# The second part of a quarter of the FFN's gate and up weights: an accumulating DMA from SBUF to SBUF in place of a DVE subtract

## The chip, the cores and the metric

The program runs on one core of a Trainium2 chip. The metric is device time in microseconds of one execution. A core has TensorE (PE in the profile; its weight loads are listed as PEld), VectorE (DVE), ScalarE (ACT), GpSimd (POOL) and SyncE (SP). SP and POOL issue DMAs, all of which run on the core's 16 DMA engines.

## The reference

One decoder layer on 256 tokens of 2048 features in float32. Cut to its flow:

```python
proj = rms_norm(x, norm1_w) @ w_in                 # q, k, v, xr, yr, g_att, g_lru
att = attention(q, k, v)                           # 16 heads of 128, one block of 256 keys, causal
lru = rglru_branch(xr, yr, ...)                    # conv, gates, a scan over tokens
merged = sigmoid(g_att) * (att @ w_proj_attn) + sigmoid(g_lru) * (lru @ w_proj_lru)
x = x + merged @ w_out
h2 = rms_norm(x, norm2_w)
x = x + (silu(h2 @ w_ffn_gate) * (h2 @ w_ffn_up)) @ w_ffn_down     # 2048 -> 5632 -> 2048
```

## The kernel before

Every projection is computed from two parts of each operand: a first part rounded to the type `float32r`, and a second part that holds what the rounding left. Three of the four products of parts are formed (first by first, first by second, second by first) and added in PSUM.

The weights stream from HBM in pieces of 512 rows by 512 columns (1 MB), in the order of their use: 292 pieces, numbered from 0. SP loads a piece into one of four buffers `w_raw` (line 101). Pieces 160 to 247 are the FFN's gate and up weights, 22 blocks of 512 columns with four pieces each, gate and up blocks in turn; pieces 248 to 291 are the down weights.

Each piece is split in two halves (`s` = 0 and 1: its first and last 256 rows) by `split`. For a half, ACT writes the first part to `w_hi` (line 107), and DVE subtracts it from the raw weights to give the second part `w_lo` (line 108). `w_hi` and `w_lo` have four buffers each, given out in turn, two to a piece. So a piece takes the buffers of the piece two before it, and each becomes free when TensorE has used it for the last time.

From piece 48 on, the products are formed with the weight's parts stationary (`features_first`, lines 661 and 662). One piece is sixteen pairs of matmuls: the first part of the weight against both parts of the activations (512 columns), then its second part against their first part (256 columns):

```python
for g in range(2):
    mine = [(k, f) for k in range(KT) for f in fs if f // 2 == g]
    for k, f in mine:
        hi, lo = (p[:, k % 2, f * P:(f + 1) * P] for p in parts[n][k // 2])
        ...
        pe.matmul(o, hi, a[:, :, k, :], ...)
        pe.matmul(o[:, 0, :], lo, a[:, 0, k, :], ...)
```

With four row chunks k and four column groups f, two of them for each g, pairs 1 to 4 use half 0, pairs 5 to 8 half 1, pairs 9 to 12 half 0 and pairs 13 to 16 half 1.

The order on each engine is the order in which this code is written. The loop over pieces writes, for piece n: SP's load of piece n + 3, the split of piece n + 1, the matmuls of piece n, and then work that is due beside the projections (a list of tasks with due times in pieces): evacuating PSUM (lines 304 and 305), the SiLU and its product (lines 602 to 616), the parts of the result `mid` (lines 297 and 298), and norms. A load waits until the raw buffer's last reader is done. GpSimd has next to no work in the FFN: four stores of the first residual sum to HBM (`x1d`, line 584) just before and at the beginning, and two small operations of the second norm (lines 192 and 193).

Of the kernel before, what the change touches and what calls it, by code (L numbers as in the profile page):

```python
# [10 lines left out]
F32 = mybir.dt.float32  # L11
F32R = mybir.dt.float32r
AF = mybir.ActivationFunctionType
OP = mybir.AluOpType
# [8 lines left out]
EPS = 1e-6  # L23
CB = 512          # columns of one block of a projection
KT = 4            # chunks of 128 rows in one loaded piece of a weight
NB = D // CB
NF = DFF // CB
SCALE = HD ** -0.5
MASKED = 1e30

# columns of `vecs`, 16 each (feature = column * 128 + partition)
V_N1, V_N2, V_CW, V_CB, V_BA, V_BX, V_LAM = 0, 16, 32, 96, 112, 128, 144
V_QN, V_KN = 160, 161
NV = 162


@with_exitstack
def layer(ctx: ExitStack, tc: tile.TileContext, x, xT, vecs, w_in, w_rg_a, w_rg_x,
# [16 lines left out]

# [1 line left out]
    pieces = []     # (source, first row chunk, first column)  # L57

# [3 lines left out]

    plan = []       # (kind, index, source of the left operand)

# [25 lines left out]
    raw, parts = {}, {}  # L90
# [19 lines left out]
    def split(n, step=2):  # L110
        if n >= len(pieces):
            return
        parts[n] = []
        for s in range(2):
            r = raw[n][:, 2 * s:2 * s + 2, :]
            hi = wp.tile([P, 2, CB], F32R, name="w_hi", bufs=4)
            lo = wp.tile([P, 2, CB], F32R, name="w_lo", bufs=4)
            parts[n].append((hi, lo))
            if step == 2:
                halves_of(r, hi, lo)  # L120
        if step == 2:
            del raw[n]

# [1 line left out]
    first = const.tile([P, 1], F32, name="first")  # L125
# [10 lines left out]

# [1 line left out]
    hT = [act_block(f"h{c}", "hT") for c in range(NB)]  # L138
# [14 lines left out]

    # the first pieces come chunk by chunk, so that TensorE starts early
    src0 = load(0)
# [14 lines left out]

    # identity, distances
    ones = const.tile([P, P], F32, name="ones")
# [16 lines left out]
    def rsqrt_mean(name, ss, n, width, where=small):  # L189
        """(ss / n + EPS) ** -0.5"""  # L190
        r = where.tile([P, width], F32, name=name)
        pool.tensor_scalar(r, ss, 1.0 / n, EPS, op0=OP.mult, op1=OP.add)
        pool.tensor_tensor(r, r, mhalf[:, :width], op=OP.pow)
        return r
# [3 lines left out]
    def rows_of(r):  # L198
        """[token, half] -> [128 times the same, token]: a task for TensorE, then a copy"""
        box = const.tile([P, T], F32, name="rb")  # L200

        def on_pe():
            t = aux()
            for h in range(2):
                pe.transpose(t[:, h * P:(h + 1) * P], r[:, h:h + 1].to_broadcast([P, P]), ident)
            later(1, lambda: act.activation(box, t[:, :T], AF.Copy))
        later(1, on_pe, True)
        return box

    def square(c, src, tags, name):  # L210
        """adds the squares of a block to those of the blocks before; the last leads to the norm"""
        if c == 0:
            st["sq"] = feat_tile(tags[0], "sq", tags[2])
            act.activation(st["sq"], src, AF.Square)
        else:
            q = feat_tile(tags[1], "sqj", tags[2])
            act.activation(q, src, AF.Square)
            dve.tensor_tensor(st["sq"], st["sq"], q, op=OP.add)
        if c == NB - 1:
            norm(name)  # L220
# [19 lines left out]

    # softplus(-lambda) = max(-lambda, 0) + 2 atanh(e / (2 + e)), e = exp(-|lambda|)
    cpos = const.tile([P, 16], F32, name="cpos")
# [20 lines left out]

# [1 line left out]
    tasks = []      # [slot, order, on TensorE, function]  # L265
    now = [0]
    order = [0]
# [18 lines left out]
    def transposed(src):  # L286
        """[token, half, 512 features] -> PSUM [feature, 4, token]"""
        t = aux()
        tv = t.rearrange("p (k h t) -> p k h t", k=KT, h=2)
        for k in range(KT):  # L290
            for h in range(2):
                pe.transpose(tv[:, k, h, :], src[:, h, k * P:(k + 1) * P], ident)  # L292
        return t

    def parts_of(dst, src):
        """dst [128, 2, 4, 256] from src [128, 4, 256]"""
        act.activation(dst[:, 0], src, AF.Copy)
        later(1, lambda: dve.tensor_tensor(dst[:, 1], src, dst[:, 0].bitcast(F32), op=OP.subtract))

    def gather(acc, dst, then):  # L300
        """dst [128, 4, 256] from the two sums of each feature"""
        def half(g):
            d = dst[:, 2 * g:2 * g + 2]
            act.activation(d, acc[g][:, :, 1, :], AF.Copy)
            dve.tensor_tensor(d, acc[g][:, :, 0, :], d, op=OP.add)
        later(0, lambda: half(0))
        later(1, lambda: (half(1), then()))
# [15 lines left out]

# [1 line left out]
    def qk_done(kind, b, acc):  # L325
# [37 lines left out]
    def scores(b):  # L363
# [44 lines left out]
        def turn(z, pair):  # L408
            t = aux().rearrange("p (a n) -> p a n", a=2)
            for a in range(2):  # L410
                hd = 2 * pair + a
                # keys of the first half: queries of both halves; keys of the second: queries of it
                pe.transpose(t[:, a, :P], z[:, hd, :P], ident)  # L413
                pe.transpose(t[:, a, P:2 * P], z[:, hd, P:2 * P], ident)  # L414
                pe.transpose(t[:, a, 2 * P:3 * P], z[:, hd, 2 * P:], ident)  # L415
# [28 lines left out]

# [1 line left out]
    sg = {}  # L446
# [32 lines left out]

# [1 line left out]
    lru = {}  # L481

    def xr_done(b, acc):
# [53 lines left out]
        def factor(g, at):  # L537
            # 1 - a^2 = tanh(-log a) (1 + a^2)
            dve.tensor_tensor(g[:, 0], at[:, 0], at[:, 0], op=OP.mult)
            dve.scalar_tensor_tensor(at[:, 1], g[:, 0], 1.0, at[:, 1], op0=OP.add, op1=OP.mult)  # L540
            dve.tensor_tensor(u, u, g[:, 1], op=OP.mult)
            later(1, lambda: act.activation(at[:, 1], at[:, 1], AF.Sqrt))
            later(2, lambda: scan(at))
# [20 lines left out]

# [1 line left out]
    x1d = dram.tile([P, NB, KT, T], F32, name="x1d")  # L566
# [26 lines left out]

# [1 line left out]
    ff = {}  # L595
# [43 lines left out]

# [1 line left out]
    def tokens_first(acc, a, n, first, last):  # L641
        """acc [token, half, column]: the left operand's parts are stationary"""
        for k in range(KT):
# [8 lines left out]
    def features_first(acc, a, n, first, last, fs=range(KT)):  # L652
        """acc[g] [column, 2, 2, token]: the weight's parts are stationary; its first part meets both parts
        of the activations in one product, and the two sums are added in the end"""
        for g in range(2):
# [84 lines left out]
```

## Time and profile before

| | |
|---|---|
| time of three runs | median 1689.32 us (1688.47 to 1690.04) |
| the profiled execution: its span, first to last instruction (the page gives no other time of it) | 1686.6 us |
| PE busy, instructions | 1676.7 us (99%), 9276 |
| PEld busy | 1455.4 us (86%) |
| DVE busy | 1040.0 us (62%) |
| ACT busy | 827.9 us (49%) |
| POOL busy | 27.7 us (2%) |
| moved by DMA | 320.30 MB, mean 190 GB/s |

Busy time says how long an engine had an instruction running. A busy engine is not by that the bound: the chain that ended last and the idle time before each group of instructions say who waits for whom. A DMA's time from issue to landing is listed for each issuing line. The DMA share is the mean busy share of the 16 engines.

### The profile page before, as it was taken

How to read it: one execution, taken by the hardware profiler on the slowest of the kernel's cores; microseconds unless marked ns; L12 is line 12 of the kernel's file. 1: busy time of each engine (PE TensorE's matmuls, PEld its weight loads, DVE VectorE, ACT ScalarE, POOL GpSimd, SP SyncE). 2: the span in 40 equal slices, each digit the busy share in tenths (PEclk: the TensorE clock that was granted, in tenths of full speed). 3: DMA queues.
4: the chain of work that ended last, by engine and by line, in shares of the span. 5: the costliest groups of instructions: out<-in, count | busy, mean ns of one | idle time of the engine just before them, and what ended most of it. 6: DMA issues, size and time to landing. Idle time of an engine off the chain costs nothing.

```text
span 1686.6 us, 22468 instructions
## 1 busy us (share of the span) xinstructions
PE 1676.7 (99%) x9276; PEld 1455.4 (86%) x9276; DVE 1040.0 (62%) x1064; ACT 827.9 (49%) x960; POOL 27.7 (2%) x35
## 2 busy tenths in 40 slices
PE   8999999999999999999999999999999999999999
PEld 6888888888888888888888888888888888888887
DVE  6565656655556867768666656666666666554444
ACT  6544554544445665756445444444444444443332
POOL 0100101000000000000000000000000000000000
PEclk9999999999999999999999999999999999999999
DMA  8554545555555555555557655555556555565662
GB/s 306 190 179 155 177 169 174 170 173 182 190 198 175 187 184 203 187 175 177 198 188 245 216 189 186 200 180 194 192 184 199 181 193 192 184 223 188 213 218 82
DMA packets 166294, 320.30 MB, mean 190 GB/s; under 512 B 5296, under 2 KB 15664, under 8 KB 166192
## 3 DMA queue, kind: packets, MB, share of 16 engines
q1 hardware_dynamic: 165328, 316.51, 55.6%
q0 software_dynamic: 576, 2.10, 0.3%
q8 instruction: 72, 1.18, 0.3%
q10 hardware_dynamic: 288, 0.26, 0.0%
q14 instruction: 30, 0.25, 0.0%
HBM read 314.66 MB, written 4.19 MB: 189 GB/s over the span
## 4 chain that ended last, share of the span: by engine, by line
PE 99%; DMA 0%; ACT 0%; SPq 0%; DVE 0%; issue 0%
PE acc L661 53%; PE acc L662 27%; PE acc L649 5%; PE acc L650 5%; PE acc L648 5%; PE aux L515 1%; PE aux L292 0%; PE aux L372 0%; PE aux L431 0%; DMA xc<-in_xT 0%; PE aux L433 0%; PE aux L371 0%; PE aux L415 0%; PE aux L413 0%; PE aux L414 0%; SPq L158 0%
## 5 line engine op out<-in xcount | busy, mean ns | idle before, releaser
L108 DVE TENSOR_TENSOR w_lo<-w_raw,w_hi 128x1024 fp32r<-128x1024 f32 (+1 forms) x586 | 711.9, 1221 | 575.8 <-ACT w_hi L107 575.7
L107 ACT ACTIVATE w_hi<-w_raw 128x1024 fp32r<-128x1024 f32 (+1 forms) x586 | 619.0, 1058 | 757.0 <-PE acc L661 548.5
L661 PE MATMUL acc<-h2T,w_hi 128*128 128x512 f32 x1408 | 488.9, 392 | 0.0
L662 PE MATMUL acc<-h2T,w_lo 128*128 128x256 f32 x1408 | 394.3, 280 | 0.0
L661 PE MATMUL acc<-hT,w_hi 128*128 128x512 f32 x1024 | 360.9, 397 | 0.0
L661 PEld LDWEIGHTS acc<-h2T,w_hi 128*128 128x128 f32 x1408 | 263.4, 187 | 58.1
L662 PE MATMUL acc<-hT,w_lo 128*128 128x256 f32 x1024 | 286.3, 280 | 0.0
L662 PEld LDWEIGHTS acc<-h2T,w_lo 128*128 128x128 f32 x1408 | 266.1, 189 | 0.0
L661 PE MATMUL acc<-mid,w_hi 128*128 128x512 f32 x704 | 244.1, 391 | 0.0
L661 PEld LDWEIGHTS acc<-hT,w_hi 128*128 128x128 f32 x1024 | 192.1, 188 | 45.2
L662 PE MATMUL acc<-mid,w_lo 128*128 128x256 f32 x704 | 197.1, 280 | 0.0
L662 PEld LDWEIGHTS acc<-hT,w_lo 128*128 128x128 f32 x1024 | 193.2, 189 | 0.3
L648 PE MATMUL acc<-w_hi,hT 128*128 128x512 f32 x384 | 153.9, 401 | 5.5 <-ACT w_hi L107 5.4
L661 PEld LDWEIGHTS acc<-mid,w_hi 128*128 128x128 f32 x704 | 131.6, 187 | 28.9
L649 PE MATMUL acc<-w_lo,hT 128*128 128x512 f32 x384 | 151.0, 393 | 0.8 <-DVE w_lo L108 0.8
L650 PE MATMUL acc<-w_hi,hT 128*128 128x512 f32 x384 | 150.7, 392 | 0.0
L662 PEld LDWEIGHTS acc<-mid,w_lo 128*128 128x128 f32 x704 | 133.1, 189 | 0.0
L648 PEld LDWEIGHTS acc<-w_hi,hT 128*128 128x128 f32 x384 | 72.8, 190 | 20.9 <-ACT w_hi L107 6.5
L661 PE MATMUL acc<-attT,w_hi 128*128 128x512 f32 x256 | 90.5, 399 | 0.0
L661 PE MATMUL acc<-merged,w_hi 128*128 128x512 f32 x256 | 90.5, 399 | 0.0
L661 PE MATMUL acc<-lruT,w_hi 128*128 128x512 f32 x256 | 90.3, 398 | 0.1
L649 PEld LDWEIGHTS acc<-w_lo,hT 128*128 128x128 f32 x384 | 72.7, 189 | 16.5 <-DVE w_lo L108 2.0
(166 smaller groups left out, 1303.8 us busy)
## 6 DMA issues: line engine op xcount, KB each, us to landing
w_raw<-in_w_in SPq DMA_DIRECT2D x110, 1024.0 KB, 5.0
w_raw<-in_w_ffn_gate SPq DMA_DIRECT2D x44, 1024.0 KB, 5.0
w_raw<-in_w_ffn_up SPq DMA_DIRECT2D x44, 1024.0 KB, 5.0
w_raw<-in_w_ffn_down SPq DMA_DIRECT2D x44, 1024.0 KB, 5.0
w_raw<-in_w_proj_attn SPq DMA_DIRECT2D x16, 1024.0 KB, 5.0
w_raw<-in_w_proj_lru SPq DMA_DIRECT2D x16, 1024.0 KB, 4.9
w_raw<-in_w_out SPq DMA_DIRECT2D x16, 1024.0 KB, 5.1
xb<-in_xT SPq DMA_DIRECT2D x4, 512.0 KB, 7.9
```

Of the source, the lines that this page charges most:

```text
L107: act.activation(hi, r, AF.Copy)
L108: dve.tensor_tensor(lo, r, hi.bitcast(F32), op=OP.subtract)
L515: pe.matmul(t[:, n * T:(n + 1) * T], wg[:, i, n, :], u[:, n, :], start=True, stop=True, skip_group_check=True)
L648: pe.matmul(o, ah, hi, start=(first and k == 0), stop=False)
L649: pe.matmul(o, ah, lo, start=False, stop=False)
L650: pe.matmul(o, al, hi, start=False, stop=(last and k == KT - 1))
L661: pe.matmul(o, hi, a[:, :, k, :], start=start, stop=False, skip_group_check=True)
L662: pe.matmul(o[:, 0, :], lo, a[:, 0, k, :], start=False, stop=stop, skip_group_check=True)
```

## The change

In `split`, the odd-numbered pieces of the gate and up weights (44 of 88) are handled differently. Their half 1 comes first, before half 0, also in the order in which buffers are given out. For half 1, ACT writes the rounded weights with the sign reversed into `w_lo`, then the rounded weights into `w_hi`; then GpSimd issues a DMA that adds the raw weights to `w_lo` (source and destination both in SBUF, 128 partitions of 4 KB). The result is raw minus rounded, as before. Half 0 of these pieces and all other pieces are handled as before. Comments were taken out of the file, and some lines have other numbers: ACT's copy and DVE's subtract are now lines 108 and 109, the two new copies lines 123 and 124, the new DMA line 125.

```diff
+FIRST_FFN = (7 * NB + 3 * NB) * 4
...
     def split(n, step=2):
         if n >= len(pieces):
             return
-        parts[n] = []
-        for s in range(2):
+        parts[n] = [None, None]
+        beside = FIRST_FFN <= n < FIRST_FFN + 2 * NF * KT and n % 2 == 1
+        for s in (1, 0) if beside else (0, 1):
             r = raw[n][:, 2 * s:2 * s + 2, :]
             hi = wp.tile([P, 2, CB], F32R, name="w_hi", bufs=4)
             lo = wp.tile([P, 2, CB], F32R, name="w_lo", bufs=4)
-            parts[n].append((hi, lo))
-            if step == 2:
+            parts[n][s] = (hi, lo)
+            if beside and s == 1:
+
+                act.activation(lo, r, AF.Copy, scale=-1.0)
+                act.activation(hi, r, AF.Copy)
+                pool.dma_start(lo.bitcast(F32), r, accum_op=OP.add)
+            elif step == 2:
                 halves_of(r, hi, lo)
```

On ACT, this is the stretch around the first up block in the kernel before. `fu` and `fg` are copies out of PSUM, `fs` is the sigmoid, `mid` the first part of a result:

```order
L304 ACTIVATE fu<-acc 128x512
L107 ACTIVATE w_hi<-w_raw 128x1024 x2
L304 ACTIVATE fu<-acc 128x512
L603 ACTIVATE fs<-fg 128x1024
L107 ACTIVATE w_hi<-w_raw 128x1024 x6
L297 ACTIVATE mid<-fu 128x1024
L304 ACTIVATE fg<-acc 128x512
```

The same stretch of ACT with the change:

```order
L311 ACTIVATE fu<-acc 128x512
L123 ACTIVATE w_lo<-w_raw 128x1024
L124 ACTIVATE w_hi<-w_raw 128x1024
L108 ACTIVATE w_hi<-w_raw 128x1024
L311 ACTIVATE fu<-acc 128x512
L610 ACTIVATE fs<-fg 128x1024
L108 ACTIVATE w_hi<-w_raw 128x1024 x2
L123 ACTIVATE w_lo<-w_raw 128x1024
L124 ACTIVATE w_hi<-w_raw 128x1024
L108 ACTIVATE w_hi<-w_raw 128x1024 x3
L304 ACTIVATE mid<-fu 128x1024
L311 ACTIVATE fg<-acc 128x512
```

An odd piece now has three copies on ACT in place of two, and the first of them (line 123) is the one that the new DMA waits for.

On POOL, the end of the program in the kernel before has the last operations of the query and key norms (`rq`), the four stores and the second norm (`rstd`):

```order
L192 TENSOR_SCALAR rq<-ss 128x8
L193 TENSOR_TENSOR rq<-rq,mhalf 128x8
L584 DMA x1d<-xb 128x1024 x4
L192 TENSOR_SCALAR rstd_7744<-ss_7742 128x2
L193 TENSOR_TENSOR rstd_7744<-rstd_7744,mhalf 128x2
```

The same stretch of POOL with the change:

```order
L591 DMA x1d<-xb 128x1024 x3
L125 DMA w_lo<-w_raw 128x1024
L591 DMA x1d<-xb 128x1024
L125 DMA w_lo<-w_raw 128x1024
L199 TENSOR_SCALAR rstd_7746<-ss_7744 128x2
L200 TENSOR_TENSOR rstd_7746<-rstd_7746,mhalf 128x2
L125 DMA w_lo<-w_raw 128x1024 x42
```

Two of the 44 new DMAs stand ahead of the second norm's operations, the first of them ahead of the last store.

## Rows read from the trace of the kernel before

**Rows 1.** The page: busy time of the engines, and for 40 equal slices of the span the granted clock of TensorE and the DMA engines' busy share, in tenths.

```profile
PE 1676.7 (99%) x9276; PEld 1455.4 (86%) x9276; DVE 1040.0 (62%) x1064; ACT 827.9 (49%) x960; POOL 27.7 (2%) x35
...
PEclk9999999999999999999999999999999999999999
DMA  8554545555555555555557655555556555565662
```

**Rows 2.** The page: shares of the chain that ended last, by engine and by line.

```profile
PE 99%; DMA 0%; ACT 0%; SPq 0%; DVE 0%; issue 0%
PE acc L661 53%; PE acc L662 27%; PE acc L649 5%; PE acc L650 5%; PE acc L648 5%; PE aux L515 1%; PE aux L292 0%; PE aux L372 0%; PE aux L431 0%; DMA xc<-in_xT 0%; PE aux L433 0%; PE aux L371 0%; PE aux L415 0%; PE aux L413 0%; PE aux L414 0%; SPq L158 0%
```

**Rows 3.** Busy time of each engine (with its instructions) in the order PE, PEld, DVE, ACT, POOL in a stretch that holds nearly all gate and up products and the first down products (from 980 to 1480 us, 500 in all), with TensorE's granted clock, the DMA share and GB/s last.

```profile
980.00:1480.00 500.00, 500.00 (x2886) 440.86 (x2885) 311.73 (x278) 234.72 (x244) 0.00 (x0) 1.00 0.57 190
```

**Rows 4.** Groups of instructions by line and shape in the same stretch: busy us, mean ns of one, then the idle time of the engine just before them and what ended it.

```profile
L108 DVE TENSOR_TENSOR w_lo<-w_raw,w_hi 128x1024 fp32r<-128x1024 f32 x181 | 221.8, 1225 | 186.6 <-ACT w_hi L107 186.6
L107 ACT ACTIVATE w_hi<-w_raw 128x1024 fp32r<-128x1024 f32 x180 | 191.2, 1062 | 228.1 <-PE acc L661 182.4 <-issue 45.7
```

**Rows 5.** Timeline of TensorE and its weight loads at two boundaries of pieces (start us, length us, engine, line, operation): the end of piece 245 and the beginning of 246, then the beginning of piece 247 and its fifth pair.

```profile
1427.34 0.39 PE L661 MATMUL acc<-h2T,w_hi 128*128 128x512 f32 x1
1427.57 0.28 PE L662 MATMUL acc<-h2T,w_lo 128*128 128x256 f32 x1
1427.69 0.39 PE L661 MATMUL acc<-h2T,w_hi 128*128 128x512 f32 x1
...
1433.23 0.39 PE L661 MATMUL acc<-h2T,w_hi 128*128 128x512 f32 x1
...
1434.62 0.19 PEld L662 LDWEIGHTS acc<-h2T,w_lo 128*128 128x128 f32 x1
```

**Rows 6.** Timeline of ACT, DVE and SP's queue at the first of these boundaries: the split of the second half of piece 247 and the load that follows it. In brackets the idle time before and what ended it.

```profile
1427.77 1.06 ACT L107 ACTIVATE w_hi<-w_raw 128x1024 fp32r<-128x1024 f32 x1 [0.32 <-PE acc L661]
...
1428.86 1.23 DVE L108 TENSOR_TENSOR w_lo<-w_raw,w_hi 128x1024 fp32r<-128x1024 f32 x1 [0.16 <-ACT w_hi L107]
...
1430.12 0.37 SPq L101 DMA_DIRECT2D w_raw<-in_w_ffn_down  x1
```

**Rows 7.** Timeline of GpSimd's four stores to HBM and of one operation of the second norm, of SP's issues ahead of these stores, then issues with their size and the us from issue to landing: weight loads (median of 44), one store by SP at 1564.56, and GpSimd's stores issued at 953.49, 885.66 and 930.87 (that of 908.28 reads as the last).

```profile
885.66 0.74 POOL L584 DMA_DIRECT2D x1d<-xb  x1 [604.29 <-DVE xb L576]
908.28 0.54 POOL L584 DMA_DIRECT2D x1d<-xb  x1 [21.88 <-DVE xb L576]
930.87 0.53 POOL L584 DMA_DIRECT2D x1d<-xb  x1 [22.05 <-DVE xb L576]
953.49 0.53 POOL L584 DMA_DIRECT2D x1d<-xb  x1 [22.09 <-DVE xb L576]
967.72 1.16 POOL L192 TENSOR_SCALAR rstd<-ss 128x2 f32<-128x2 f32 x1 [13.70 <-ACT ss L235]
...
884.05 0.37 SPq L101 DMA_DIRECT2D w_raw<-in_w_out  x1
884.47 0.81 SPq L572 DMA_DIRECT2D xb<-in_xT  x1
...
907.10 0.49 SPq L572 DMA_DIRECT2D xb<-in_xT  x1
...
929.70 0.59 SPq L572 DMA_DIRECT2D xb<-in_xT  x1
...
951.89 0.37 SPq L101 DMA_DIRECT2D w_raw<-in_w_ffn_up  x1
...
w_raw<-in_w_ffn_gate SPq DMA_DIRECT2D x44, 1024.0 KB, 5.0
...
out<-xb SPq DMA_DIRECT2D x1, 512.0 KB, 3.3
...
x1d<-xb POOLq DMA_DIRECT2D x1, 512.0 KB, 5.2
...
x1d<-xb POOLq DMA_DIRECT2D x1, 512.0 KB, 7.9
...
x1d<-xb POOLq DMA_DIRECT2D x1, 512.0 KB, 8.0
```

**Rows 8.** DMA queues in short stretches (packets, MB, share of the 16 engines' time; q1 is SP's queue, q0 GpSimd's): all that moved from 953.49 to 956.07, the store's packets from 956 to 959, a store's share of the 10 us from 885 to 895; then the busy times of the engines from 956 to 957 with the DMA share and GB/s last.

```profile
q1 hardware_dynamic: 407, 0.83, 94.5%
...
q0 software_dynamic: 144, 0.52, 42.9%
...
q0 software_dynamic: 144, 0.52, 15.7%
...
956.00:957.00 1.00, 1.00 (x7) 0.86 (x7) 0.81 (x2) 1.00 (x4) 0.00 (x0) 1.00 1.06 424
```

**Rows 9.** Timeline of TensorE: the first matmul of the output projection (pieces 144 to 159), of the gate and up blocks (160 to 247) and of the down blocks.

```profile
859.01 0.40 PE L661 MATMUL acc<-merged,w_hi 128*128 128x512 f32 x1
...
949.47 0.40 PE L661 MATMUL acc<-h2T,w_hi 128*128 128x512 f32 x1
...
1438.78 0.39 PE L661 MATMUL acc<-mid,w_hi 128*128 128x512 f32 x1
```

**Rows 10.** What SP's queue waited for from 980 to 1480: us in total, times, longest.

```profile
SPq L101 <- DVE w_lo L108: 459.0, 90, 5.3
```

## The prediction

> **What bounds the kernel now.** I read the engines' busy shares first, then the chain that ended last, then one stretch by itself. The page shows TensorE busy for 99% of the span at full granted clock in every slice [rows 1], and the chain is TensorE from end to end, with the two matmul lines of the feature-first products making up four fifths of it [rows 2]. In the 500 us that hold nearly all of the gate and up products TensorE has no idle time at all, while DVE is busy for 312 and ACT for 235 [rows 3]. DVE's subtracts and ACT's copies there are each preceded by idle time [rows 4]. So DVE is a supplier with time to spare. Work taken off it returns nothing unless TensorE waits for it, and here TensorE does not wait.
>
> One piece takes 5.55 us: the last gate and up piece (an odd one) runs from 1433.23 to 1438.78 [rows 5, 9]. Its sixteen pairs of matmuls come 0.347 us apart. I follow this piece, called C, since its second half is one of the halves that the change touches. A is the odd piece two before it; A ends, and the even piece between begins, at 1427.69. I count from there as t = 0.
>
> **Part by part.** *Removed:* 44 DVE subtracts (88 pieces, every second one, one half of two) of 1.225 us, 53.9 us of DVE time [rows 4]. Value to the end: nothing, as TensorE was not waiting for them.
>
> *Added on ACT:* 44 copies with a scale of -1, same shape as the 1.062 us copies, 46.7 us. ACT idles before its weight copies for 228 us in the same 500 [rows 4], so the sum fits. The order matters more: for an odd piece ACT now writes -part of the second half, then its first part, then the first part of the first half. Counting 1.06 us each from t = 0.20 they end at 1.26, 2.32 and 3.38; the DVE subtract of the first half ends near 4.7. TensorE asks for that half when C begins, t = 5.55. About 0.8 us remain. Cost: 0 by this order; if ACT or DVE were held up by more than 0.8 us there, the excess would stall TensorE.
>
> *Added: the transfer, and a wait for it.* This is the term that decides. The buffer that the transfer fills was A's. It comes free when A's last matmul with a second part, the one at 1427.57 of 0.28 us, is done: t = 0.16. In the kernel before, ACT started 0.04 us after the corresponding matmul of the first part (that one starts at 1427.34 and lasts 0.39) and DVE 0.03 us after ACT [rows 5, 6]. So ACT's new copy runs from t = 0.20 to 1.26 and GpSimd can issue at t = 1.3. TensorE first needs the second half of C for its fifth pair, whose weights are loaded at 1434.62, t = 6.93 [rows 5]. The transfer may thus take 6.93 - 1.3 = 5.6 us from issue to landing. Call its real time L. If L is larger, TensorE stops once for L - 5.6, and again at each of the next ones: A's end releases the buffer, C's end releases it for the piece after next, so nothing can be made up in between. The price is 44 x (L - 5.6).
>
> The trace has no accumulating transfer, so L is bounded by the nearest rows. Below: a 512 KB store issued by SP lands after 3.3 us [rows 7]. Above: GpSimd's own 512 KB stores of the same shape land after 5.2 once and after 7.9 to 8.0 three times [rows 7, 8]. An add also reads its destination, another 0.52 MB; at the 424 GB/s of a full slice that is 1.2 us [rows 8]. The bounds are then 3.3 and 8.0 + 1.2 = 9.2, or a price of 0 and of 44 x 3.6 = 158 us. The value I take starts from the 5.2. That store was issued at 953.49; until 956.07 not one of its packets moved, and the SP queue filled 94.5% of the DMA engines with a weight load issued at 951.89 [rows 7, 8]. It waited behind a load. The slow three were issued about a microsecond after a 512 KB load as well, and the first of these came behind a weight load too. Will a load be in front of the new transfers? In this part the load of an even piece is issued when DVE has read the buffer before it, 2.43 us after a piece ends (1430.12 against 1427.69) [rows 5, 6]. For the even piece ahead of a new transfer that is t = -3.1, and at 5.0 us to landing [rows 7] it is in by t = 1.9, soon after the issue at 1.3. The load of an odd piece now waits for the new transfer itself, since that reads the raw buffer last, and so comes after it. Half of the 2.6 us of waiting should therefore go, 1.3, and the second read adds 1.2: L = 5.2 - 1.3 + 1.2 = 5.1. That is 0.5 under the limit, and I cost the transfer at nothing. The cover is thin.
>
> The Trainium skill ("DMA: Bandwidth & Descriptors", section on the anatomy of one DMA on the gpsimd path) gives 2.0 us plus bytes over 436 GB/s, and its page "Collectives: The Full Stack" (section on the bandwidth ceiling) says that an adding transfer reads two sources and so runs at half rate. By these two L would be an estimated 2.0 + 2.4 = 4.4 us and the stall 0. The measured 5.2 of a plain store is 2 us over that formula (3.2), so the trace does not agree while loads run.
>
> *Moved: the raw buffer's release.* SP's load into an odd piece's buffer went out at t = 2.43; now at 1.3 + 5.1 = 6.4. It lands 5.0 later, t = 11.4. ACT first needs it when the odd piece after C ends, t = 22.2. SP waited 459 us in 90 such waits in this part [rows 10], so it is early, and the 4 us cost nothing. *Queued behind:* on GpSimd the first two new transfers stand before the norm's two small operations at 967.72, but issue near 951 and 962. *Traffic:* one 0.52 MB store took 15.7% of the engines over 10 us, 1.6 us [rows 8]; twice that for the add, every 11.1 us, is 28% on top of 57% [rows 3]. It fits.
>
> **Sum.** 0 (DVE) + 0 (ACT) + 0 (transfer) + 0 (load). The profiled execution's span is 1686.6; the timed runs have a median of 1689.32, 2.7 more around it. I say 1689.6, the few tenths for first waits.
>
> **Rivals.**
> *B, the transfer is a little late.* L between 5.7 and 6.9. For it: my L is a difference of rows that do not show an add, and each packet must fetch two rows before it writes one. With 5.2 + 1.2 = 6.4 (no wait saved), 44 x 0.8 = 35 us; with L = 6.2, 26. Time about 1689 + 26 = 1715. It is slower from L = 5.7 on.
> *C, far late.* The transfer behaves as the three slow stores, whatever the loads do: L = 8.0, 44 x 2.4 = 106, about 1795. Against it: no other 512 KB load stands before it in this part.
> *D, TensorE restarts in a slower rhythm.* Between 859.01 and 949.47 the 256 pairs of the stage before took 0.3534 us each; piece C took 0.3467 [rows 5, 9]. Same instructions, same clock. If a short wait throws the 132 pieces from here to the end into the slower rhythm, 132 x 16 x 0.0067 = 14 us, about 1703.
> *E, GpSimd is held up by DVE while it issues.* One DVE operation lasts 1.23 us [rows 4]; L would be 5.1 + 1.2 = 6.3, 44 x 0.7 = 31 us, about 1720. Against it: DVE's next subtract waits for ACT's third copy and starts near t = 3.4, after the issue. The Trainium skill ("SBUF — State Buffer", section on the two separate sides) has this rule: a DVE instruction that takes the port shared with GpSimd keeps it from writing descriptors. No row here shows such a stall.
> *F, faster.* Only if the slower rhythm of [rows 9] ended earlier than about 20 us into this part; that is worth under 0.5 us. Nothing else of TensorE's idle lies here.
>
> **Chances.** A, hidden: 0.46. B 0.30, C 0.12, D 0.06, E 0.03, F or chance 0.03. A measurement of this kernel tells about 0.2% from no change, 3.4 us. Faster 0.03, same 0.46, slower 0.51: the slower cases together outweigh A, but each alone is less likely. The likeliest case's own range is 1687.5 to 1692.5. The range that holds 8 in 10 reaches from 1686.5 over D, E and all of B (L = 6.9 gives 57 us) to 1750 and leaves out C and F.
>
> **What the profile after would show.** Right: 44 transfers into w_lo with a median landing near 5.1 us, at most 5.6; no TensorE idle before the second-part matmuls; gate and up still 489.3 us from the first product with h2T (949.47) to the first with mid (1438.78); DVE's subtracts down by 54 us, ACT's copies up by 47; SP's load waiting for w_lo's transfer. Wrong: TensorE waiting 44 times for the transfer, by L - 5.6 each (B, C); or no wait, but pairs 0.353 apart (D); or a GpSimd issue that lasts until a DVE operation ends (E).

## The result, and the profile after

The changed kernel takes 1699.01 us (median of 3 runs, 1698.33 to 1700.97) against 1689.32: ratio 1.0062, interval 1.0046 to 1.0078. The forecast was 1689.6, its range 1686.5 to 1750. The span of the profiled execution is 1696.1, 9.5 us more than before.

From the page of the changed kernel: busy time of the engines, and of the DMA queues the packets, MB and share of 16 engines' time (q0 is GpSimd's).

```profile
PE 1685.9 (99%) x9276; PEld 1456.9 (86%) x9276; DVE 986.4 (58%) x1020; ACT 864.4 (51%) x1004; POOL 65.7 (4%) x79
...
PEclk9999999999999999999999999999999999999999
...
q0 software_dynamic: 6912, 25.17, 7.5%
...
PE 99%; DMA 0%; ACT 0%; SPq 0%; DVE 0%; issue 0%
...
w_lo<-w_raw POOLq DMA_DIRECT2D x44, 512.0 KB, 5.1
```

DVE lost 53.6 us of work, as worked out, and TensorE is the chain from end to end as in [rows 1, 2]. TensorE executes the same 9276 matmuls at the same granted clock, yet is "busy" 9.2 us longer. The new transfers land after a median of 5.1 us, the value that the prediction took. Only two of them were waited for. From the waits of the changed kernel (us in total, times, longest):

```profile
PEld acc L669 <- DMA w_lo<-w_raw: 0.5, 2, 0.2
```

Half a microsecond of waiting does not make 9.5. The timeline of TensorE at the three places of [rows 9] tells in which stage the time came:

```profile
946.28 0.39 PE L668 MATMUL acc<-h2T,w_hi 128*128 128x512 f32 x1
...
1443.60 0.40 PE L668 MATMUL acc<-mid,w_hi 128*128 128x512 f32 x1
```

| stage | before | after | difference |
|---|---|---|---|
| to the first gate product | 949.47 | 946.28 | -3.2 |
| gate and up | 489.3 | 497.3 | +8.0 |
| down, to the end of the span | 247.8 | 252.5 | +4.7 |

Of the 12.7 us lost, 4.7 lie in the down products, which have no transfer, and 3.2 us are gained in stages that the change does not touch. The groups of first-part matmuls by their left operand show what differs: busy us, then the mean ns of one. Before:

```profile
L661 PE MATMUL acc<-h2T,w_hi 128*128 128x512 f32 x1408 | 488.9, 392 | 0.0
L661 PE MATMUL acc<-mid,w_hi 128*128 128x512 f32 x704 | 244.1, 391 | 0.0
L661 PE MATMUL acc<-lruT,w_hi 128*128 128x512 f32 x256 | 90.3, 398 | 0.1
L661 PE MATMUL acc<-merged,w_hi 128*128 128x512 f32 x256 | 90.5, 399 | 0.0
```

After:

```profile
L668 PE MATMUL acc<-h2T,w_hi 128*128 128x512 f32 x1408 | 496.7, 398 | 0.0
L668 PE MATMUL acc<-mid,w_hi 128*128 128x512 f32 x704 | 248.8, 399 | 0.0
L668 PE MATMUL acc<-lruT,w_hi 128*128 128x512 f32 x256 | 88.9, 391 | 0.1
L668 PE MATMUL acc<-merged,w_hi 128*128 128x512 f32 x256 | 88.8, 391 | 0.0
```

The same instruction has a mean of about 391 ns or of about 399. These are the two rhythms of the prediction's rival D, 0.3467 and 0.3533 us a pair. In the changed kernel the gate and up products run in the first (but for 12 us, from 963 to 975, between the matmuls and the transposes of the second norm) and change to the second at 1021. Here is the timeline of TensorE at the place, and last the weight load that was late (in brackets the idle time and its releaser):

```profile
1020.84 0.39 PE L668 MATMUL acc<-h2T,w_hi 128*128 128x512 f32 x1
1021.15 0.39 PE L669 MATMUL acc<-h2T,w_lo 128*128 128x256 f32 x1
1021.37 0.39 PE L668 MATMUL acc<-h2T,w_hi 128*128 128x512 f32 x1
...
1022.07 0.40 PE L668 MATMUL acc<-h2T,w_hi 128*128 128x512 f32 x1
1022.31 0.28 PE L669 MATMUL acc<-h2T,w_lo 128*128 128x256 f32 x1
1022.43 0.40 PE L668 MATMUL acc<-h2T,w_hi 128*128 128x512 f32 x1
...
1021.15 0.19 PEld L669 LDWEIGHTS acc<-h2T,w_lo 128*128 128x128 f32 x1 [0.23 <-DMA w_lo<-w_raw]
```

The second part of piece 173 is late by 0.23 us; TensorE stops once; two pairs later the starts are 0.36 apart where they were 0.347. The groups of first-part matmuls in two windows, from 1000 to 1020 and from 1022 to 1440 us, with transfers in both:

```profile
L668 PE MATMUL acc<-h2T,w_hi 128*128 128x512 f32 x59 | 20.5, 391 | 0.0
...
L668 PE MATMUL acc<-h2T,w_hi 128*128 128x512 f32 x1184 | 418.4, 399 | 0.0
```

The first late transfer (piece 169, at 998.8 us) had also stopped TensorE for 0.2 us, and after it the first rhythm went on. So a stop does not always change the rhythm.

### The profile page after: what moved, and what is told of

It reads as the page before. It is cut to its first block, busy times and chain, and to the rows that moved or that the text cites. A ratio compares the mean times of both kernels' runs of the same rounds, so it can differ in the third digit from the quotient of the medians.

```text
span 1696.1 us, 22559 instructions
## 1 busy us (share of the span) xinstructions
PE 1685.9 (99%) x9276; PEld 1456.9 (86%) x9276; DVE 986.4 (58%) x1020; ACT 864.4 (51%) x1004; POOL 65.7 (4%) x79
## 4 chain that ended last, share of the span: by engine, by line
PE 99%; DMA 0%; ACT 0%; SPq 0%; DVE 0%; issue 0%
PE acc L668 53%; PE acc L669 27%; PE acc L656 5%; PE acc L657 5%; PE acc L655 5%; PE aux L522 1%; PE aux L299 0%; PE aux L379 0%; PE aux L438 0%; DMA xc<-in_xT 0%; PE aux L440 0%; PE aux L378 0%; PE aux L422 0%; PE aux L420 0%; PE aux L421 0%; SPq L165 0%
## 5 line engine op out<-in xcount | busy, mean ns | idle before, releaser
L109 DVE TENSOR_TENSOR w_lo<-w_raw,w_hi 128x1024 fp32r<-128x1024 f32 (+1 forms) x542 | 658.3, 1221 | 638.8 <-ACT w_hi L108 638.5
L108 ACT ACTIVATE w_hi<-w_raw 128x1024 fp32r<-128x1024 f32 (+1 forms) x542 | 571.3, 1056 | 639.7 <-PE acc L668 442.0
L668 PE MATMUL acc<-h2T,w_hi 128*128 128x512 f32 x1408 | 496.7, 398 | 0.0
L668 PE MATMUL acc<-mid,w_hi 128*128 128x512 f32 x704 | 248.8, 399 | 0.0
L123 ACT ACTIVATE w_lo<-w_raw 128x1024 fp32r<-128x1024 f32 x44 | 46.7, 1060 | 90.2 <-PE acc L669 90.2
L668 PE MATMUL acc<-merged,w_hi 128*128 128x512 f32 x256 | 88.8, 391 | 0.0
```

The source lines that it names most:

```text
L108: act.activation(hi, r, AF.Copy)
L109: dve.tensor_tensor(lo, r, hi.bitcast(F32), op=OP.subtract)
L123: act.activation(lo, r, AF.Copy, scale=-1.0)
L668: pe.matmul(o, hi, a[:, :, k, :], start=start, stop=False, skip_group_check=True)
```

## The experiments

Each run of a kernel stands beside runs of the kernel before on the same chip. With many of them it showed that the kernel before has two groups of times itself: of 60 runs on two chips 44 lie from 1684.2 to 1690.0 and 16 from 1700.8 to 1703.2, with none between; on two other chips all 30 lie from 1685.1 to 1690.4. The upper group is 13 us higher, nearly the 14 that 132 pieces in the second rhythm cost by the prediction's working. A trace of the kernel before in its upper group was not taken, so that this is its cause is likely and not shown. Ratios below are over the runs of both groups.

**The unaltered changed kernel again** (*after_again*).

> The changed kernel unaltered, to see its runs spread beside many of the kernel before, whose 25 runs so far fell in two groups (19 from 1684.2 to 1689.7, 6 from 1700.8 to 1703.2). Theory T (a stop draws the rhythm; the change adds stops): the changed kernel has the same two groups, most runs now in the upper one, at 1697 to 1705, some at 1685 to 1690. Rival R (traffic or the added ACT and GpSimd work costs some us in every run): one group, near 1699, and none below 1693.

Twelve runs: four at 1688.2 to 1690.0, eight at 1700.3 to 1703.9; the 35 runs beside them of the kernel before: 25 and 10 in the same two groups. Ratio 1.0036 (1.0005 to 1.0067). With the first three, 11 of 15 runs of the changed kernel lie at 1698 or above. In the lower group the two kernels do not differ (medians 1688.4 and 1689.2). So a run of the changed kernel can be as fast as the kernel before, and the upper group is likelier with the change (8 of 12 against 10 of 35 on this chip); rival R falls. The profiled run is one of the upper ones: it has one late transfer, for which a weight load waited 1.1 us until 1015.45, and the second rhythm from there to the end. No lower run of this kernel was traced; e11_after_rhythm below has one of the changed kernel with other edits.

**Transfers in the first 8 of the 44 pieces** (*e2_first8*).

```diff
-        beside = FIRST_FFN <= n < FIRST_FFN + 2 * NF * KT and n % 2 == 1
+        beside = FIRST_FFN <= n < FIRST_FFN + 16 and n % 2 == 1
```

> The changed kernel with the transfer only in pieces 161 to 175 (8 of 44); all later second parts by DVE. Theory T: the late transfers of pieces 169 and 173 are still there, and if the restart is again the slow one, pairs stay 0.353 apart to the end though no transfer flows after 1030: time 1697 to 1701; if the restart happens to be the fast one, 1687 to 1690. Rival R (traffic): fast rhythm from 1030 on at the latest, time 1690 at most, and never slow without transfers.

1687.93 us (1686.61 to 1703.73), ratio 1.0007 (0.9974 to 1.0040): eight runs of ten in the lower group, two at 1702 to 1704. In the profiled run the eight transfers land after 4.5 to 5.9 us, none is waited for, and the matmuls with h2T and mid have a mean of 391 ns. Not decisive alone: the late transfers that theory T counted on did not come in that run, and the two slow runs were not traced. It shows that they are no fixed property of these pieces.

**TensorE interrupted, without and with transfers** (*e3_taps_before*, *e4_taps_after*): ten one-column matmuls, whose result nobody reads.

```diff
+            if n >= 168 and n % 12 == 0 and n < 288:
+                t = aux()
+                pe.matmul(t[:, 0:1], ones, ones[:, 0:1], start=True, stop=True, skip_group_check=True)
```

> The kernel before with ten extra one-column matmuls on TensorE (behind pieces 168, 180, ... 276), which interrupt the stream for about 0.2 to 0.5 us each; no transfer at all. Theory T: each interruption draws the rhythm anew, so that some of the eleven stretches of about 12 pieces run at 0.347 and some at 0.353 us a pair; with half of them slow 2 to 5 us of stops plus about 7 us, time 1692 to 1700. Rival R: no transfers, so all stretches at 0.347, time 1691 to 1694.

> The changed kernel with the same ten extra matmuls. Theory T: the rhythm is drawn anew at each, so fast stretches appear while the transfers flow, time between 1690 and 1703. Rival R: every stretch with transfers (to piece 247) is slow, the down stretches fast, time 1700 or more.

1703.48 us (1700.24 to 1704.89) and 1703.39 (1698.48 to 1705.65), ratios 1.0082 each (1.0052 to 1.0112 and 1.0053 to 1.0112). The timeline of e3_taps_before at the first extra matmul (the kernel without transfers):

```profile
1001.61 0.28 PE L696 MATMUL aux<-ones 128*128 128x1 f32 x2
1001.75 0.48 PE L661 MATMUL acc<-h2T,w_hi 128*128 128x512 f32 x1
1002.07 0.28 PE L662 MATMUL acc<-h2T,w_lo 128*128 128x256 f32 x1
1002.18 0.40 PE L661 MATMUL acc<-h2T,w_hi 128*128 128x512 f32 x1
```

Its groups from 980 to 1000 and from 1005 to 1065 us:

```profile
L661 PE MATMUL acc<-h2T,w_hi 128*128 128x512 f32 x59 | 20.5, 391 | 0.0
...
L661 PE MATMUL acc<-h2T,w_hi 128*128 128x512 f32 x171 | 60.5, 399 | 0.0
```

One interruption of a fraction of a microsecond changes 391 ns to 399, with no transfer in the program. Both expectations missed: there is no even draw at each matmul, as theory T had it, for all ten stretches behind these matmuls are in the second rhythm, in both kernels. In each kernel only the first of the ten found TensorE in the first rhythm and changed it; the other nine found the second and left it. The traffic is not needed for the slow rhythm (the down stretches without transfers are slow too); that part of rival R is refuted here.

**Interrupted by transposes, with transfers** (*e7_after_resets*): the interruption that the second norm makes.

```diff
+            if n in (176, 200, 224, 248, 264):
+                t = aux()
+                for h in range(2):
+                    pe.transpose(t[:, h * P:(h + 1) * P], mhalf[:, h:h + 1].to_broadcast([P, P]), ident)
```

> The changed kernel with five pairs of small transposes on TensorE (behind pieces 176, 200, 224, 248 and 264), as those of the second norm near 975, after which six profiles of six went on in the fast rhythm. Theory T: the rhythm after each is drawn anew, mostly fast, so that stretches with transfers run at 0.347 us a pair after 176, and the down products too: time 1687 to 1695. Rival R: stretches up to piece 247 stay at 0.353: time 1697 or more.

1695.6 us (1689.4 to 1703.82), ratio 1.0021 (0.9993 to 1.0049). The runs now fill the gap between the two groups, as they would if stretches of both kinds are mixed. The profiled run does so. The second norm's own transposes, at 978, were followed by the second rhythm here. From 1002, where a transfer was late by 0.1 us, the first rhythm holds, and the transposes at 1044 and 1178 leave it so. From 1280 the second rhythm holds, from the transposes at 1312 the first, from 1348 to 1381 once more the second, and then the first to the end. Of the five inserted pairs only that at 1312 found the second rhythm, and it ended it. The groups from 1050 to 1170 and from 1282 to 1310 us:

```profile
L668 PE MATMUL acc<-h2T,w_hi 128*128 128x512 f32 x347 | 120.3, 391 | 0.0
...
L668 PE MATMUL acc<-h2T,w_hi 128*128 128x512 f32 x81 | 28.7, 399 | 0.0
```

With 391 ns through 120 us in which eleven transfers ran, the traffic does not keep TensorE slow. At 1280 no wait is listed. The transfer issued at 1272.78 landed 6.7 us later, at 1279.5, and the rhythm changes there. The timeline shows the weight load that needs this transfer:

```profile
1279.55 0.39 PE L668 MATMUL acc<-h2T,w_hi 128*128 128x512 f32 x1
1279.57 0.19 PEld L669 LDWEIGHTS acc<-h2T,w_lo 128*128 128x128 f32 x1
```

It starts 0.02 us after the matmul ahead of it, where in the 100 us before such a load starts within 0.003 us of its matmul. The changes at 1347 and 1381 stand at loads of this kind too, late by 0.1 us each. So delays far below the listed waits go with a change.

**Half 1 multiplied last in odd pieces** (*e1_half1_last*).

```diff
-        for g in range(2):
-            mine = [(k, f) for k in range(KT) for f in fs if f // 2 == g]
+        beside = FIRST_FFN <= n < FIRST_FFN + 2 * NF * KT and n % 2 == 1
+        for ks, g in [((0, 1), 0), ((0, 1), 1), ((2, 3), 0), ((2, 3), 1)] if beside else \
+                [(range(KT), 0), (range(KT), 1)]:
+            mine = [(k, f) for k in ks for f in fs if f // 2 == g]
```

> The changed kernel, but in the 44 odd gate and up pieces TensorE takes all pairs of half 0 first and those of half 1 last, so that the transfer is needed at pair 9 in place of pair 5, 1.39 us later. Theory T (two waits of 0.2 us for late transfers stopped TensorE, and the restart threw it into the slower rhythm, which then lasts): no wait for a transfer, pairs 0.347 us apart through gate, up and down, gate and up 489 us, time 1686 to 1690. Rival R (the transfers' traffic itself keeps TensorE slow while they flow): 44 transfers as before, gate and up 497 us, time 1695 or more.

A miss: 1702.54 us (1695.32 to 1705.41), ratio 1.0066 (1.0034 to 1.0097). It was meant to take the waits away and made more of them. The waits of this kernel:

```profile
PEld acc L671 <- DMA w_lo<-w_raw: 7.2, 11, 1.2
PE acc L671 <- DMA w_lo<-w_raw: 3.9, 6, 0.9
```

From the page, the time to landing of its 44 transfers (the median), and from the DMA queues for 3 us from the issue of one of them at 1130.42:

```profile
w_lo<-w_raw POOLq DMA_DIRECT2D x44, 512.0 KB, 8.6
...
q1 hardware_dynamic: 600, 1.20, 105.9%
```

Issued at another moment of the piece, the transfers fall behind SP's weight loads: for 3 us only q1 moves. The eleven listed waits of weight loads come to 7.2 us (the 3.9 of the matmuls behind them are part of the same stops), and still its gate and up matmuls have a mean of 393 ns, most of them in the first rhythm, while the last stop, at 1409, left all of down at 399. So even 44 transfers of 8.6 us do not slow the matmuls; late ones cost their wait and then what the rhythm after it costs.

**Halves in their usual order** (*e5_half_order*).

```diff
-        for s in (1, 0) if beside else (0, 1):
+        for s in (0, 1):
```

> The changed kernel, but an odd piece's halves are split in the order 0, 1 as all others. By the prediction's account of the buffers this changes nothing for the transfer's buffer (free when the piece two before has ended), and only ACT's copy of half 0 comes first. If the buffer of half 1 was in truth that of half 0 in the changed kernel (free 1.39 us earlier), the order 0, 1 takes this away: the issue moves to 1.3 us after the piece's end, 5.6 us remain, and TensorE waits for all transfers that take longer, 10 or more waits, time 1700 to 1720.

1699.25 us (1689.48 to 1701.95), ratio 1.0040 (1.0014 to 1.0065). Six waits, 4.3 us of weight loads late and 2.4 of matmuls. The ACT copies and TensorE in this kernel:

```profile
1059.24 1.06 ACT L108 ACTIVATE w_hi<-w_raw 128x1024 fp32r<-128x1024 f32 x1 [0.67 <-PE acc L668]
1060.74 1.06 ACT L123 ACTIVATE w_lo<-w_raw 128x1024 fp32r<-128x1024 f32 x1 [0.44 <-PE acc L669]
...
1068.08 0.39 PE L669 MATMUL acc<-h2T,w_lo 128*128 128x256 f32 x1 [0.22 <-DMA w_lo<-w_raw]
```

Half 0's copy is released at three quarters of the piece before the last, and the copy for the transfer 1.50 later, at its end. Expected were 10 waits or more and 1700 us or more; six in the profile is fewer, but more than the two of the changed kernel, and the moment of release is the one claimed.

The profiled runs with late transfers (the changed kernel, after_again, e1, e5, e7) list 21 waits of weight loads for them. 18 of these found TensorE in the first rhythm: 12 were followed by the first rhythm again and 6 by the second. The 3 that found the second left it. The length did not decide it: e5's wait of 2.0 us at 1092 is among the 12, the changed kernel's of 0.2 us at 1021 among the 6. So a late transfer puts TensorE into the slower rhythm sometimes, about once in three, and not mostly.

**A transfer for the last 128 rows alone** (*e6_last_chunk*).

```diff
-                act.activation(lo, r, AF.Copy, scale=-1.0)
+                act.activation(lo[:, 1], r[:, 1], AF.Copy, scale=-1.0)
                 act.activation(hi, r, AF.Copy)
-                pool.dma_start(lo.bitcast(F32), r, accum_op=OP.add)
+                pool.dma_start(lo[:, 1].bitcast(F32), r[:, 1], accum_op=OP.add)
+                dve.tensor_tensor(lo[:, 0], r[:, 0], hi[:, 0].bitcast(F32), op=OP.subtract)
```

> The changed kernel, but only the last 128 rows of each odd piece come by the transfer (256 KB in place of 512, needed at pair 7 in place of 5); DVE makes the other 128. Theory T: transfers land in 3.5 to 5 us, no wait of TensorE, so the runs fall as those of the kernel before do, most at 1684 to 1690. Rival R (traffic): half of the transfers' traffic, so half of the loss, 1692 to 1695.

1688.75 us (1687.72 to 1702.96), ratio 0.9983 (0.9951 to 1.0014). Nine of ten runs in the lower group. The 44 transfers land after 3.3 to 6.2 us, median 4.3, and none is waited for. Needed two pairs later and shorter, the transfer costs nothing that these runs can tell.

**What the rhythm is worth** (*e9_before_rhythm*, *e10_chunk_rhythm*, *e11_after_rhythm*): on the kernel before, on e6_last_chunk and on the changed kernel, transposes as in e7 behind three pieces, and one stop of TensorE less.

```diff
+            if n in (60, 114, 176):
+                t = aux()
+                for h in range(2):
+                    pe.transpose(t[:, h * P:(h + 1) * P], mhalf[:, h:h + 1].to_broadcast([P, P]), ident)
...
-            later(1, lambda: halves_of(s, lruT[b][:, 0], lruT[b][:, 1]))
+            if b == NB - 1:
+                halves_of(s, lruT[b][:, 0], lruT[b][:, 1])
+            else:
+                later(1, lambda: halves_of(s, lruT[b][:, 0], lruT[b][:, 1]))
```

> The kernel before (no transfer), with three pairs of small transposes on TensorE, behind pieces 60, 114 and 176, where the slow rhythm held in all profiles (from 351 and from 675 us) or was drawn at the second norm (975), and with the last block's parts of lruT made one piece earlier, which takes away TensorE's 0.4 us wait near 785 us. Theory T (the rhythm follows the last interruption): stretches 370 to 525, 690 to 737 and 785 to 966 run at 0.347 in place of 0.353 us a pair, worth 2.9, 0.9 and 3.4 us, against 3 x 0.6 us for the transposes; the runs near 1702 become rarer; median 1682 to 1686. Rival R2 (the rhythm belongs to the stage and its operands, not to the interruption): same stretches as before, time 1690 to 1692.

> The same two edits on the kernel in which only the last 128 rows of an odd piece come by the transfer. Theory T: no late transfer, so the same time as the kernel before with these edits, within 1 us. Rival R (a transfer costs time by its traffic): 3 us or more above it.

> The changed kernel with the edits of e9_before_rhythm: what the whole transfers do when nothing else disturbs the rhythm. Theory T (late transfers stop TensorE, a stop mostly ends in the slow rhythm): unlike e9 and e10, whose runs all lie from 1682.7 to 1685.0, most runs lie 5 to 15 us higher, some without a late transfer at 1683 to 1686; median 1690 to 1698. Rival R3 (what spread the runs was the second norm's interruption alone, and late transfers matter little): all runs at 1683 to 1686, as in e9.

e9_before_rhythm: 1683.21 us (1682.70 to 1684.99), ratio 0.9973 (0.9962 to 0.9983). This beats both kernels. Its groups by left operand, to be read beside the 398 and 399 of before:

```profile
L664 PE MATMUL acc<-attT,w_hi 128*128 128x512 f32 x256 | 88.8, 391 | 0.0
L664 PE MATMUL acc<-lruT,w_hi 128*128 128x512 f32 x256 | 88.8, 394 | 0.0
L664 PE MATMUL acc<-merged,w_hi 128*128 128x512 f32 x256 | 88.8, 394 | 0.0
```

The 394 is a third pattern at the pace of the first: from 760 to 958 the first-part matmuls last 395 and 392 ns by turns and start 0.350 and 0.343 us apart, so a pair still takes 0.3467 and the stage 88.8 us. Its timeline at the first transposes (L700); the mean of one first-part matmul is 399 ns from 370 to 378 us and 391 from 382 to 430:

```profile
378.29 0.40 PE L664 MATMUL acc<-hT,w_hi 128*128 128x512 f32 x1
378.52 0.28 PE L665 MATMUL acc<-hT,w_lo 128*128 128x256 f32 x1
378.64 0.38 PE L700 MATMUL aux<-ident,mhalf 128*128 128x128 f32 x2
378.78 0.48 PE L664 MATMUL acc<-hT,w_hi 128*128 128x512 f32 x1
379.10 0.29 PE L665 MATMUL acc<-hT,w_lo 128*128 128x256 f32 x1
379.22 0.39 PE L664 MATMUL acc<-hT,w_hi 128*128 128x512 f32 x1
```

Rival R2, a rhythm that belongs to a stage, falls. The three stages take 1.5 to 1.7 us less each, 4.9 together, about the 5.1 by which the span fell (1681.5). Two edits were made at once: attT runs right behind the first transposes, while lruT and merged stand where the stop near 785 us was taken away. e10_chunk_rhythm, with 44 transfers of half the size: 1683.37 (1683.05 to 1684.54), ratio 0.9972 (0.9961 to 0.9984), the same. e11_after_rhythm, on another chip: five runs at 1683.6 to 1685.7 and seven from 1689.4 to 1695.1, median 1689.43, ratio 1.0007 (0.9993 to 1.0020). Its median is 0.6 us under the range that theory T gave. Rival R3 (all runs at 1683 to 1686) falls. The five lower runs carry all 44 whole transfers and are within 1 us as fast as e9_before_rhythm, so neither the transfers' traffic nor ACT's third copy costs more than that by itself. The profiled run is one of the lower ones: its transfers land after at most 6.8 us, none is waited for. That late transfers lie behind the higher runs agrees with all other traces; no trace of a higher run of this kernel was taken.

## Why the prediction came out as it did

*The number.* 1699.01 lies in the stated range, but not in the likeliest case's own (1687.5 to 1692.5). It is there because the wide range spans D, which had a chance of 0.06.

*The bound, DVE and ACT.* Right. TensorE is the chain, DVE lost 53.6 us (53.9 worked out), and none of it returned. ACT's busy time rose by 36.5 us (46.7 worked out): of two copies in a row the second starts before the first has ended, by 0.10 us at 1013.69. The first half of the odd pieces was never late.

*The median of L.* Right: 5.1. The terms behind it are right in kind: GpSimd's queue takes 7.5% of the engines' time after and 0.3% before, so (0.075 x 1696.1 - 0.003 x 1686.6) / 44 = 2.8 us of all 16 engines for one transfer, against 0.003 x 1686.6 / 4 = 1.3 for a plain store of the same size (1.6 by [rows 8]). The sum had put twice a store's share into the traffic (3.1). This agrees with the rule of the Trainium skill ("Collectives: The Full Stack", section on the bandwidth ceiling) that an adding transfer reads two sources and runs at half rate.

*"The load of an odd piece now waits for the new transfer itself, and so comes after it."* This step failed. It comes after that transfer, but before the next one, and together with the even piece's load it is still in the queue then. The two loads ahead of the late transfer of piece 173, the transfer and its landing, then the queues from 1014.08 to 1016.08, in which only SP's moves, and from 1016.08 to 1017.60, in the changed kernel:

```profile
1009.11 0.37 SPq L102 DMA_DIRECT2D w_raw<-in_w_ffn_up  x1
1010.79 0.37 SPq L102 DMA_DIRECT2D w_raw<-in_w_ffn_gate  x1
...
1014.08 0.85 POOL L125 DMA_DIRECT2D w_lo<-w_raw  x1 [10.24 <-ACT w_lo L123]
...
w_lo<-w_raw POOLq DMA_DIRECT2D x1, 512.0 KB, 7.0
...
q1 hardware_dynamic: 332, 0.68, 95.2%
...
q0 software_dynamic: 49, 0.20, 66.0%
q1 hardware_dynamic: 138, 0.25, 43.1%
```

The transfer's first packet moves 2.0 us after its issue, and then shares the engines with the rest of the load. Where only the even load stands ahead (the transfer issued at 1115.84, which landed after 4.5) it is 1.4 us; in e1_half1_last's transfer of 1130.42 it is 3.5. A later landing makes the next odd load later (that of 1009.11 goes out as the transfer before has landed) and so the next transfer too. L was therefore not one number near 5.1 but ran from 4.5 to 7.0. The Trainium skill ("DMA: Bandwidth & Descriptors", section on queues, rings and completion order) has the engines take turns between queues packet by packet. This trace agrees in that both queues move for the 1.5 us behind the first packet, at 66% and 43% of the engines' time; whether they alternate packet by packet was not examined, and what holds the first packet back behind the loads was not shown.

*"TensorE ... may thus take 5.6 us."* Also wrong, on the safe side. The buffer given to the transfer is that of half 0, not half 1: ACT's copy starts at 1012.73, right behind the last pair with half 0, and A ends at 1013.91. From the issue at 1014.08 to the weight load that was due at 1020.85 there are 6.8 us. Half 1 is split first in odd pieces and so gets the buffer that comes free first; e5_half_order takes that back. Transfers of 7.0 missed 6.8 by 0.2. The price of rival B, 44 equal stops, came in no run: 12 of the 44 transfers took more than 5.6 us here, of which two were waited for, and in e5_half_order, which has the window of 5.6, six took longer and six waits are listed.

*The sum of 0 and case A (0.46).* The transfer was hidden but for 0.5 us in the profiled run, and the kernel was yet 9.7 us slower (medians). What was mis-sized is the chance of D, 0.06. Its condition (a short wait), its mechanism (the pairs go on 0.353 apart to the end) and its price (14 us; measured +12.7 in gate, up and down, from 1020 on) came as worked out. I had weighed a wait and the rhythm as separate cases, when B's small wait is what sets off D, about once in three waits. Why one stop ends in the second rhythm and another does not stays open. The -3.2 us before gate and up are the same thing with the other sign: TensorE waits 0.4 us for lruT near 785 in both traces, and happened to go on in the first rhythm after it in the changed kernel. That is luck; without it the changed kernel would have stood near 1702.

*Rival C and E.* No transfer took 8 us in the changed kernel, and the GpSimd issues last 0.85 to 0.92 us each, with no stall.

## What to carry to other kernels

Where TensorE is the chain, read the mean duration of one and the same matmul by stage: a step between two values at one granted clock stood at an interruption of the stream in these traces, and one wait of 0.2 us was followed by a loss of sixty times its length (12.7 us). Work taken off an engine that nobody waits for is worth nothing, and what it is replaced by must arrive with more room than its median, since a transfer that shares the DMA engines with large loads waits for those in front (here 4.5 to 7.0 us around a median of 5.1). Before a difference under 1% is explained, take enough runs to see whether the kernel before has one group of times or two.

## What the runs showed of the hardware that I had not expected

- The stream of paired matmuls (512 and 256 columns, weights loaded for each) runs in one of two rhythms, 0.3467 or 0.3533 us a pair, at granted clock 1.00 in both, and keeps it over hundreds of microseconds until it is interrupted; a weight load 0.02 us late was enough (e7).
- The kind of interruption matters: a one-column matmul was followed by the second rhythm in 20 stretches of 20 (e3, e4; 18 of them were in it already); a pair of small transposes inserted behind a piece by the first in 14 of 14 (five in e7, three each in e9, e10 and e11; seven found the second). The second norm's own transposes and waits for data went either way. Why is open.
- A transfer added from SBUF to SBUF by GpSimd's queue lands after 4.5 us at best for 512 KB, and after up to 10.2 us behind two loads of 1 MB (e1).
